# First FFN products of a hybrid decoder block: plain copies out of PSUM, and the row factor of x2 moved into a lane beside the next weights

## The chip, the core and the metric

The kernel runs on one core of a Trainium2 chip. The metric is the device time of one execution in microseconds. In the text PE is the matrix engine (TensorE), DVE the VectorE, ACT the ScalarE, POOL the GpSimd and SP the engine that issues most DMAs. The five engines run their own instruction streams in order and wait for each other through semaphores.

## What is computed

One layer of a decoder block on 256 rows of width 2048, fp32: a hybrid token mixer, cross-attention into 256 memory rows, and a gated MLP (FFN). Each has an RMSNorm before and after. The change lies where the second sub-layer ends and the FFN begins:

```python
x = x + rmsnorm(y, g[3])          # x2, end of the cross-attention
h = rmsnorm(x, g[4])
up = h @ w_up                      # 2048 x 11264
conv = conv_b + sum(up_pad[:, j:j + s] * conv_w[j] for j in range(3))
gate, val = jnp.split(conv, 2, axis=-1)
y = (jax.nn.gelu(gate) * val) @ w_down
x = x + rmsnorm(y, g[5])
```

The row factor of `rmsnorm(x, g[4])` is one number for each row, and `h @ w_up` is linear in the rows, so the kernel multiplies by it after the matmul.

## The kernel before

**Numbers and weights.** A weight block of 4 x 128 rows and 256 columns is loaded by SP into one of four `raw` buffers (512 KB). ACT makes the high half `hi` of it (L234, a cast) and DVE the rest `lo` (L236, a subtraction); both have three buffers. A product is then `hi` times x's high half, `hi` times x's low half and `lo` times x's high half. `split` gives these two instructions a high priority.

**The end of x2.** The four column chunks of x2 (tiles `row`) are finished by DVE (L1337). As they come, `transposed` turns each into `h3T` (tiles `h`): PE transposes into the PSUM tiles `auxp` and `auxq` (L389), ACT scales the high half out (L375), DVE the low half (L376). The row factor isn't in `h3T`. `row_factors` makes it: eight squares with row sums on ACT (L409), a reduce and a scaling on DVE (L412, L413), a power on POOL (L414). `over_rows` spreads it over all partitions: a small matmul on PE (L421) and a copy by DVE into `rrow` (L424), which the code calls `x2row`. The squares are pinned behind the last high half of `h3T`.

**The first FFN products.** `wstat_first` makes the first gate block and the first value block together, in all four banks of the PSUM tag `mm` (two row tiles each), with 192 matmuls of 256 columns at L287. It takes `h3T` step by step as the transposes give it. All later blocks come from `wstat2`, 16 steps for each of two row tiles: one matmul of 512 columns (L302) and one of 256 (L304) a step, in two banks. Call such a couple of matmuls a pair.

**Emptying the banks.** `conv` multiplies a product by `x2row` into `z` and applies the width-3 convolution, with one ACT and two DVE instructions (L1484, L1485, L1487). For the first two blocks the multiplication reads PSUM itself (L1479), so each of the four banks is held until `x2row` exists. For later blocks the two halves of a bank are added first (an ACT copy at L1481 and a DVE addition at L1482) and POOL multiplies by `x2row` (L1483). The gate goes through Gelu (L1497), is multiplied by the value (L1502) and split into `hid` (L1505, L1506).

**What sets the order.** The program is written in one stream; a scheduler of the framework orders each engine's instructions from it, with priorities (`tc.high_priority`). A `Lanes` object `L` holds generators: `L.add` puts work in, and the loops over weights call `L.advance`, which lets a lane issue its next piece behind the matmul just written (`tc.issue_after`). Before the change no lane runs during the FFN.

Of the kernel before, what the change touches and what calls it, by code (L numbers as in the profile page):

```python
# [15 lines left out]
AF = mybir.ActivationFunctionType  # L16
# [4 lines left out]
P = 128  # L21
D = 2048
S = 256
# [149 lines left out]
def hybrid_block(tc, a, out, dbg=None):  # L173
    nc = tc.nc
    dbg = dbg or {}
    with ExitStack() as ctx:
# [14 lines left out]
        def mk(pool, tag, bufs, shape=(P, 512), dt=F32):  # L191
            t = pool.tile(list(shape), dt, tag=tag, bufs=bufs, name=nm(tag))
            return t
# [207 lines left out]

        def row_factors(src, tmp, pins=(None,) * 4):

            r = mk(cp, "rs", 3, (P, 2))
            part = mk(cp, "rpart", 2, (P, 8))
            for c in range(4):
                with tc.issue_after(pins[c].ins) if pins[c] else ExitStack():
                    for t in range(2):
                        nc.scalar.activation(tmp(), src[t][c], AF.Square,  # L409
                                             accum_out=part[:, 4 * t + c:4 * t + c + 1])  # L410
            ss = small(2)
            nc.vector.tensor_reduce(ss, part.rearrange("p (t c) -> p t c", t=2), axis=AX.X, op=ALU.add)  # L412
            nc.vector.tensor_scalar(ss, ss, 1.0 / D, 1e-6, op0=ALU.mult, op1=ALU.add)  # L413
            last_pow[0] = nc.gpsimd.tensor_tensor(r, ss, mhalf[:, :2], op=ALU.pow)  # L414
            return r
# [1049 lines left out]
                    nc.sync.dma_start(dbg["x2"][t * P:(t + 1) * P, c * 512:(c + 1) * 512], x2[t][c])  # L1465


        x2row = over_rows(row_factors(x2, xtmp, (h3T.last,) * 4))
        right2.close()
        mixer.close()  # L1470
        ffn = ExitStack()
# [4 lines left out]
        def conv(ps, dst, n):  # L1476
            z = mk(fp, "z", 4, (P, S))
            if ps.shape[1] == S:
                nc.vector.tensor_tensor(z, ps, x2row, op=ALU.mult)  # L1479
            else:  # L1480
                nc.scalar.copy(z, ps[:, S:])  # L1481
                nc.vector.tensor_tensor(z, ps[:, :S], z, op=ALU.add)  # L1482
                nc.gpsimd.tensor_tensor(z, z, x2row, op=ALU.mult)  # L1483
            nc.scalar.activation(dst, z, AF.Identity, bias=cw[:, 3, n:n + 1], scale=cw[:, 2, n:n + 1])  # L1484
            nc.vector.scalar_tensor_tensor(dst[:, 1:], z[:, :S - 1], cw[:, 1, n:n + 1], dst[:, 1:],  # L1485
                                           op0=ALU.mult, op1=ALU.add)
            nc.vector.scalar_tensor_tensor(dst[:, 2:], z[:, :S - 2], cw[:, 0, n:n + 1], dst[:, 2:],  # L1487
                                           op0=ALU.mult, op1=ALU.add)

        hid = Packed(2)  # L1490
        first = wstat_first(w_up, (0, D_FF), 256, h3T)
        for j in range(FT // 2):
            g = mk(fp, "gv", 4)
            ps = wstat2(w_up, j * 256, 256, h3T) if j else first[0]
            for t in range(2):
                conv(ps[t], g[:, t * S:(t + 1) * S], 2 * j + t)
            nc.scalar.activation(g, g, AF.Gelu_apprx_tanh)  # L1497
            v = mk(fp, "gv", 4)
            ps = wstat2(w_up, D_FF + j * 256, 256, h3T) if j else first[1]
            for t in range(2):  # L1500
                conv(ps[t], v[:, t * S:(t + 1) * S], FT + 2 * j + t)
            nc.vector.tensor_tensor(v, v, g, op=ALU.mult)  # L1502
            hi = mk(fp, "hid", FT, dt=F32R)
            lo = mk(fp, "hid", FT, dt=F32R)
            nc.scalar.copy(hi, v)  # L1505
            nc.vector.tensor_tensor(lo, v, hi.bitcast(F32), op=ALU.subtract)  # L1506
            hid.hi.append(view(hi, k=2, t=S))
            hid.lo.append(view(lo, k=2, t=S))

        gb5 = bcast_row(gains[5], hbuf32)  # L1510

# [33 lines left out]
```

## Time and profile before

| | us |
|---|---|
| median of 3 runs | 1355.32 |
| lowest and highest of them | 1351.33, 1360.78 |
| the profiled execution, its own time | 1363.17 |
| span of its profile, first to last instruction | 1361.4 |
| PE busy | 1325.9 |
| DVE busy | 874.0 |
| ACT busy | 707.3 |

A row of the timeline gives the start, the time until the end, the engine and line, the tile written and the tiles read, the number of instructions merged, and in brackets how long the engine was idle before and what released it. Matmuls overlap, so PE's rate is read from the distance of starts. PEclk is the share of full clock that PE was granted: 1.00 is 2.4 GHz and 0.50 is 1.2 GHz. Times are from the start of the span. The FFN's first matmul starts at 604.77 us, and the last FFN matmul at about 1353 us.

### The profile page before, as it was taken

The numbers are of one execution on the slowest core, as the hardware profiler recorded it, in microseconds if no ns is written. First come the engines' busy times: TensorE is split into PE (matmuls) and PEld (weight loads), VectorE is DVE, ScalarE is ACT, GpSimd is POOL, SyncE is SP. The second block draws the span as 40 slices with busy tenths as digits, with TensorE's granted clock in tenths as the row PEclk, the third lists the DMA queues.
The fourth block names the chain that finished last, engine by engine and source line by source line (L and its number), as shares of the span: only waits on it lengthen the run. The fifth ranks groups of instructions, "written<-read, shape, count | busy, mean of one in ns | idle before, by whom it ended". The sixth has DMA issues, their size and how long they took to land.

```text
span 1361.4 us, 20945 instructions
## 1 busy us (share of the span) xinstructions
PE 1325.9 (97%) x8184; PEld 1160.2 (85%) x8184; DVE 874.0 (64%) x1298; ACT 707.3 (52%) x1075; POOL 141.6 (10%) x179
## 2 busy tenths in 40 slices
PE   6899999999999999989999999999999999999997
PEld 6889979989977889778888888888888888888886
DVE  6579964466775765566766767676767674444444
ACT  6755363244456654556555555555555553434442
POOL 3010101200013100000111111111111120000000
PEclk9999999999999999998999999999999999999999
DMA  7545553155558755444666566666666666666663
GB/s 236 143 138 156 148 171 101 48 178 155 148 162 298 232 178 174 155 124 140 184 186 187 186 186 186 186 185 186 186 186 186 187 217 198 191 196 192 195 194 132
DMA packets 189841, 238.82 MB, mean 175 GB/s; under 512 B 7920, under 2 KB 144013, under 8 KB 189741
## 3 DMA queue, kind: packets, MB, share of 16 engines
q1 hardware_dynamic: 185514, 225.23, 53.6%
q0 software_dynamic: 3376, 11.29, 2.5%
q8 instruction: 64, 1.05, 0.3%
q10 hardware_dynamic: 851, 0.95, 0.2%
q14 instruction: 36, 0.29, 0.1%
HBM read 235.33 MB, written 2.12 MB: 174 GB/s over the span
## 4 chain that ended last, share of the span: by engine, by line
PE 92%; DVE 2%; issue 2%; DMA 2%; ACT 1%; POOL 1%; ACTq 0%; SPq 0%; DVEq 0%; POOLq 0%
PE mm L302 23%; PE mm L304 12%; PE mm L324 11%; PE mm L330 11%; PE mm L326 11%; PE mm L271 5%; PE mm L266 5%; PE mm L268 5%; PE mm L287 1%; DMA wa<-in_rwkv_w_up_dram 1%; PE auxq L675 1%; DVE lo L236 1%; ACT hi L234 1%; PE auxp L1073 0%; PE auxq L933 0%
## 5 line engine op out<-in xcount | busy, mean ns | idle before, releaser
L236 DVE TENSOR_TENSOR lo<-raw,hi 128x1024 fp32r<-128x1024 f32 x422 | 519.6, 1233 | 380.8 <-ACT hi L234 378.9
L234 ACT CAST hi<-raw 128x1024 fp32r<-128x1024 f32 x422 | 442.9, 1050 | 452.8 <-PE mm L302 170.0
L302 PE MATMUL mm<-h,hi 128*128 128x512 f32 x1344 | 477.6, 400 | 2.4 <-DVE z L1479 2.4
L304 PE MATMUL mm<-h,lo 128*128 128x256 f32 x1344 | 378.7, 282 | 0.0
L302 PEld LDWEIGHTS mm<-h,hi 128*128 128x128 f32 x1344 | 253.9, 189 | 66.1 <-issue 2.5
L304 PEld LDWEIGHTS mm<-h,lo 128*128 128x128 f32 x1344 | 255.3, 190 | 0.0
L266 PE MATMUL mm<-h,hi 128*128 128x256 f32 x592 | 153.1, 290 | 0.0
L268 PE MATMUL mm<-h,hi 128*128 128x256 f32 x592 | 150.5, 286 | 0.0
L324 PE MATMUL mm<-hi,hid 128*128 128x512 f32 x352 | 137.0, 389 | 0.0
L326 PE MATMUL mm<-hi,hid 128*128 128x512 f32 x352 | 136.9, 389 | 0.0
L266 PEld LDWEIGHTS mm<-h,hi 128*128 128x128 f32 x592 | 113.9, 193 | 2.6 <-issue 1.5
L268 PEld LDWEIGHTS mm<-h,hi 128*128 128x128 f32 x592 | 113.8, 193 | 0.4 <-issue 0.3
L1483 POOL TENSOR_TENSOR z<-z,rrow 128x256 f32<-128x256 f32 x84 | 69.1, 823 | 412.1 <-DVE z L1482 412.1
L330 PE MATMUL mm<-lo,hid 128*128 128x512 f32 x352 | 108.4, 389 | 0.0
L271 PE MATMUL mm<-h,lo 128*128 128x256 f32 x592 | 97.5, 285 | 0.0
L271 PEld LDWEIGHTS mm<-h,lo 128*128 128x128 f32 x592 | 82.5, 192 | 1.3 <-DVE lo L236 0.6
L324 PE MATMUL mm<-hi,h 128*128 128x512 f32 (+1 forms) x208 | 79.2, 386 | 1.7 <-ACT hi L234 1.7
L326 PEld LDWEIGHTS mm<-hi,hid 128*128 128x128 f32 x352 | 66.1, 188 | 13.8
L330 PEld LDWEIGHTS mm<-lo,hid 128*128 128x128 f32 x352 | 66.1, 188 | 13.7
L324 PEld LDWEIGHTS mm<-hi,hid 128*128 128x128 f32 x352 | 66.0, 188 | 13.7
L326 PE MATMUL mm<-hi,h 128*128 128x512 f32 (+1 forms) x208 | 77.0, 375 | 0.0
L330 PE MATMUL mm<-lo,h 128*128 128x512 f32 (+1 forms) x208 | 59.8, 375 | 0.2 <-DVE lo L236 0.2
(347 smaller groups left out, 1545.2 us busy)
## 6 DMA issues: line engine op xcount, KB each, us to landing
raw<-in_ffn_w_up_dram SPq DMA_DIRECT2D x176, 512.0 KB, 4.6
raw<-in_w_in_dram SPq DMA_DIRECT2D x94, 512.0 KB, 4.3
raw<-in_ffn_w_down_dram SPq DMA_DIRECT2D x88, 512.0 KB, 4.9
raw<-in_w_out_dram SPq DMA_DIRECT2D x32, 512.0 KB, 4.7
raw<-in_mem_wkv_dram SPq DMA_DIRECT2D x16, 512.0 KB, 3.5
raw<-in_mem_wq_dram SPq DMA_DIRECT2D x8, 512.0 KB, 3.4
raw<-in_mem_wo_dram SPq DMA_DIRECT2D x8, 512.0 KB, 3.7
x<-in_x_dram SPq DMA_DIRECT2D x8, 256.0 KB, 6.8
```

What stands on the lines that cost most here:

```text
L234: nc.scalar.copy(hv, rv)
L236: nc.vector.tensor_tensor(lv, rv, hv.bitcast(F32), op=ALU.subtract)
L266: nc.tensor.matmul(o, lhsT=hv[:, k, cs], rhs=X.h(k0 + k), start=(k0 + k == 0), stop=False)
L268: nc.tensor.matmul(o, lhsT=hv[:, k, cs], rhs=X.l(k0 + k), start=False, stop=False)
L271: L.last = nc.tensor.matmul(o, lhsT=lv[:, k, cs], rhs=X.h(k0 + k), start=False, stop=(k0 + k == nk - 1))
L287: L.last = nc.tensor.matmul(ps[g][t][:, :S], lhsT=w[:, k, cs], rhs=x(k0 + k), start=(k0 + k == 0 and i == 0), stop=(k0 + k == KT - 1 and i ...
L302: nc.tensor.matmul(view(ps[t], z=2, t=S), lhsT=hv[:, k, cs], rhs=X.hl[k0 + k], start=(k0 + k == 0), stop=False)
L304: L.last = nc.tensor.matmul(ps[t][:, S:], lhsT=lv[:, k, cs], rhs=X.h(k0 + k), start=False, stop=(k0 + k == KT - 1))
L324: nc.tensor.matmul(o, lhsT=X.h(kk)[:, ts_], rhs=hv[:, k, :], start=(first and k0 + k == 0), stop=False)
L326: nc.tensor.matmul(o, lhsT=X.l(kk)[:, ts_], rhs=hv[:, k, :], start=False, stop=False)
L330: L.last = nc.tensor.matmul(o, lhsT=X.h(kk)[:, ts_], rhs=lv[:, k, :], start=False, stop=(last and k0 + k == nk - 1))
L1483: nc.gpsimd.tensor_tensor(z, z, x2row, op=ALU.mult)
```

## The change

`row_factors` is cut in two, so that `factors_of` (reduce, scaling, power) can follow squares made elsewhere. The eight squares of x2, the factor, `over_rows` and the whole first gated tile (`conv` of four products, Gelu, product, split) become a lane, `second_norm` with `first_hidden`, which is added before `wstat_first` and drained after the first `wstat2` block. The squares write their unused output into one tile `junk` of the FFN's pool instead of four rotating ones. The four products of `wstat_first` are copied from PSUM to new tiles `zf`, two by ACT and two by DVE, without the factor; `conv` then multiplies `zf` by the factor in SBUF. The arithmetic is the same.

```diff
         def row_factors(src, tmp, pins=(None,) * 4):
-            r = mk(cp, "rs", 3, (P, 2))
             part = mk(cp, "rpart", 2, (P, 8))
...
+            return factors_of(part)
+
+        def factors_of(part):
+            r = mk(cp, "rs", 3, (P, 2))
             ss = small(2)
...
-        x2row = over_rows(row_factors(x2, xtmp, (h3T.last,) * 4))
+        rpart = mk(cp, "rpart", 2, (P, 8))
+
+        def second_norm():
+
+            junk = mk(fp, "gv", 4)
+            for c in range(4):
+                for t in range(2):
+                    nc.scalar.activation(junk, x2[t][c], AF.Square, accum_out=rpart[:, 4 * t + c:4 * t + c + 1])
+                yield 2.2
+            got["x2row"] = over_rows(factors_of(rpart))
+            yield 1.0
+            yield from first_hidden()
...
         def conv(ps, dst, n):
             z = mk(fp, "z", 4, (P, S))
             if ps.shape[1] == S:
-                nc.vector.tensor_tensor(z, ps, x2row, op=ALU.mult)
+                nc.vector.tensor_tensor(z, ps, got["x2row"], op=ALU.mult)
...
-        first = wstat_first(w_up, (0, D_FF), 256, h3T)
-        for j in range(FT // 2):
-            g = mk(fp, "gv", 4)
-            ps = wstat2(w_up, j * 256, 256, h3T) if j else first[0]
...
+        def first_hidden():
+            gv = [mk(fp, "gv", 4) for _ in range(2)]
+            for n in range(2):
+                for t in range(2):
+                    conv(got["first"][n][t], gv[n][:, t * S:(t + 1) * S], n * FT + t)
+                yield 1.5
+            nc.scalar.activation(gv[0], gv[0], AF.Gelu_apprx_tanh)
+            hidden(0, *gv)
+
+        L.add(second_norm())
+        first = wstat_first(w_up, (0, D_FF), 256, h3T)
+        with tc.high_priority(offset=2 * AHEAD):
+            got["first"] = [[mk(fp, "zf", 4, (P, S)) for _ in range(2)] for _ in range(2)]
+            for n in range(2):
+                for t in range(2):
+                    copy2(t, got["first"][n][t], first[n][t])
+        for j in range(1, FT // 2):
+            g = mk(fp, "gv", 4)
+            ps = wstat2(w_up, j * 256, 256, h3T)
+            if j == 1:
+                L.drain(lambda: not L.lanes)
```

`copy2` is an older helper: a DVE copy (L733 of the new file) where its first argument is odd, an ACT copy (L735) where it is even.

What the scheduler makes of it, first on PE where `wstat_first` ends and the first `wstat2` block begins. Before (`auxp` with `rs` is `over_rows`; `mm_6444` to `mm_6447` are the four first products, and `mm_6717` takes the bank of `mm_6444`):

```order
L287 MATMUL mm_6447<-h_6407,hi_6636 128x256 x2
L287 MATMUL mm_6447<-h_6407,lo_6637 128x256
L421 MATMUL auxp_6434<-ident,rs_6412 128x128 x2
L302 MATMUL mm_6717<-h_6323,hi_6721 128x512
L304 MATMUL mm_6717<-h_6323,lo_6722 128x256
```

The same place of the changed kernel (`mm_6418` to `mm_6421` are the first products, and `mm_6680` and `mm_6681` take the banks of the first two):

```order
L287 MATMUL mm_6421<-h_6407,lo_6618 128x256
L302 MATMUL mm_6680<-h_6323,hi_6684 128x512
L304 MATMUL mm_6680<-h_6323,lo_6685 128x256
...
L302 MATMUL mm_6681<-h_6337,hi_6684 128x512
L304 MATMUL mm_6681<-h_6337,lo_6685 128x256
L424 MATMUL auxp_6709<-ident,rs_6704 128x128 x2
L302 MATMUL mm_6680<-h_6347,hi_6716 128x512
```

The matmul of `over_rows` (now L424) has moved behind the first eight pairs of the next block.

On DVE at the same place, before (`small` is the factor on its way, `rrow` its spread form):

```order
L236 TENSOR_TENSOR lo_6722<-raw_6719,hi_6721 128x1024
L412 TENSOR_REDUCE small_6430<-rpart_6413 128x2
L413 TENSOR_SCALAR small_6430<-small_6430 128x2
L236 TENSOR_TENSOR lo_6744<-raw_6741,hi_6743 128x1024
L236 TENSOR_TENSOR lo_6766<-raw_6763,hi_6765 128x1024
L424 COPY rrow_6437<-auxp_6434 128x256
L1479 TENSOR_TENSOR z_6689<-mm_6444,rrow_6437 128x256
```

And on DVE after:

```order
L236 TENSOR_TENSOR lo_6685<-raw_6682,hi_6684 128x1024
L415 TENSOR_REDUCE small_6705<-rpart_6412 128x2
L416 TENSOR_SCALAR small_6705<-small_6705 128x2
L733 COPY zf_6672<-mm_6419 128x256
L733 COPY zf_6674<-mm_6421 128x256
L236 TENSOR_TENSOR lo_6717<-raw_6714,hi_6716 128x1024
L236 TENSOR_TENSOR lo_6751<-raw_6748,hi_6750 128x1024
L427 COPY rrow_6712<-auxp_6709 128x256
L236 TENSOR_TENSOR lo_6783<-raw_6780,hi_6782 128x1024
L1494 TENSOR_TENSOR z_6730<-zf_6671,rrow_6712 128x256
```

The DVE copies stand behind the reduce, and the multiplication by the factor stands behind the low halves of the next block.

On ACT, after, where the squares end (before, all eight squares stood behind the last `h` row, with two casts behind the second of them; two now stand ahead of that row):

```order
L375 ACTIVATE h_6407<-auxq_6401,gpar 128x256
L1478 ACTIVATE gv_6482,rpart_6412<-row_6204 128x512
L1478 ACTIVATE gv_6482,rpart_6412<-row_6208 128x512
L234 CAST hi_6617<-raw_6615 128x1024
L234 CAST hi_6684<-raw_6682 128x1024
...
L1478 ACTIVATE gv_6482,rpart_6412<-row_6306 128x512
L735 COPY zf_6671<-mm_6418 128x256
L234 CAST hi_6716<-raw_6714 128x1024
L735 COPY zf_6673<-mm_6420 128x256
```

The first ACT copy stands behind all eight squares, with nothing between it and the last of them.

## Rows read from the trace of the kernel before

**Rows 1.** The page's head and its row of PE: span, and PE's busy time with its share of the span.

```profile
span 1361.4 us, 20945 instructions
PE 1325.9 (97%) x8184; PEld 1160.2 (85%) x8184; DVE 874.0 (64%) x1298; ACT 707.3 (52%) x1075; POOL 141.6 (10%) x179
```

**Rows 2.** All waits of PE from 604 us to the end of the span: who waited for whom, us in total, times, longest.

```profile
PE auxp L389 <- DVE row L1337: 2.9, 1, 2.9
PE mm L302 <- DVE z L1479: 2.4, 1, 2.4
PE auxp L421 <- POOL rs L414: 0.5, 1, 0.5
PE mm L287 <- ACT h L375: 0.3, 1, 0.3
```

**Rows 3.** Timeline of PE where the first FFN products end and the next block begins.

```profile
631.91 0.40 PE L287 MATMUL mm<-h,hi 128*128 128x256 f32 x2
632.15 0.28 PE L287 MATMUL mm<-h,lo 128*128 128x256 f32 x1
632.92 0.71 PE L421 MATMUL auxp<-ident,rs 128*128 128x128 f32 x4 [0.49 <-POOL rs L414]
636.01 0.77 PE L302 MATMUL mm<-h,hi 128*128 128x512 f32 x1 [2.38 <-DVE z L1479]
636.78 0.63 PE L302 MATMUL mm<-h,hi 128*128 128x512 f32 x1
...
641.91 0.48 PE L302 MATMUL mm<-h,hi 128*128 128x512 f32 x1
...
642.35 0.40 PE L302 MATMUL mm<-h,hi 128*128 128x512 f32 x1
...
643.75 0.40 PE L302 MATMUL mm<-h,hi 128*128 128x512 f32 x1
```

**Rows 4.** Busy time of each engine in stretches (columns: stretch and its length, PE, PEld, DVE, ACT, POOL busy with instructions, then PEclk, DMA share, GB/s): around the pause of rows 3, and two stretches earlier in the FFN's first products.

```profile
605.00:610.00 5.00, 5.00 (x32) 5.00 (x33) 2.92 (x6) 1.79 (x4) 0.00 (x0) 0.71 0.16 56
620.00:625.00 5.00, 4.90 (x41) 4.70 (x40) 4.01 (x7) 3.51 (x8) 0.00 (x0) 1.00 0.37 113
...
634.00:635.00 1.00, 0.00 (x0) 0.00 (x0) 1.00 (x2) 0.00 (x0) 0.00 (x0) 1.00 0.05 9
635.00:636.00 1.00, 0.00 (x0) 0.02 (x1) 0.97 (x4) 0.05 (x1) 0.00 (x0) 0.63 0.68 172
636.00:637.00 1.00, 0.99 (x3) 0.91 (x4) 0.94 (x4) 1.00 (x3) 0.00 (x0) 0.50 1.04 352
...
641.00:642.00 1.00, 1.00 (x5) 0.85 (x4) 0.00 (x0) 0.71 (x1) 0.00 (x0) 0.50 0.00 0
642.00:643.00 1.00, 1.00 (x7) 0.86 (x7) 0.63 (x1) 0.98 (x2) 0.00 (x0) 0.96 0.00 0
```

**Rows 5.** Timeline of ACT from the last steps of `h3T` to the first convolution: the transposed halves, the squares with the reading of their sums, the casts.

```profile
616.95 0.47 ACT L375 ACTIVATE h<-auxq,gpar 128x256 fp32r<-128x256 f32 x1
619.36 1.05 ACT L234 CAST hi<-raw 128x1024 fp32r<-128x1024 f32 x1 [1.94 <-issue]
...
624.42 0.47 ACT L375 ACTIVATE h<-auxq,gpar 128x256 fp32r<-128x256 f32 x1 [1.08 <-DVE h L376]
624.79 0.62 ACT L409 ACTIVATE tmp<-row 128x512 f32<-128x512 f32 x1
625.31 0.19 ACT L409 ACTIVATION_READ_ACCUMULATOR tmp<-row 128x1 f32 x1
625.40 0.62 ACT L409 ACTIVATE tmp<-row 128x512 f32<-128x512 f32 x1
...
631.50 0.19 ACT L409 ACTIVATION_READ_ACCUMULATOR tmp<-row 128x1 f32 x1
631.63 1.99 ACT L234 CAST hi<-raw 128x1024 fp32r<-128x1024 f32 x2
```

**Rows 6.** Timeline of DVE from the reduce of the squares to the first multiplication by the factor.

```profile
631.72 0.16 DVE L412 TENSOR_REDUCE small<-rpart 128x2 f32<-128x8 f32 x1 [2.28 <-ACT tmp L409]
...
632.71 2.36 DVE L236 TENSOR_TENSOR lo<-raw,hi 128x1024 fp32r<-128x1024 f32 x2 [0.62 <-ACT hi L234]
634.99 0.42 DVE L424 COPY rrow<-auxp 128x256 f32<-128x256 f32 x1
635.44 1.09 DVE L1479 TENSOR_TENSOR z<-mm,rrow 128x256 f32<-128x256 f32 x3
```

**Rows 7.** Groups of instructions from 660 to 1000 us, the steady FFN: line, engine, operation, tiles and shapes, count, busy us, mean ns of one, idle time before and its releaser.

```profile
L302 PE MATMUL mm<-h,hi 128*128 128x512 f32 x964 | 340.7, 399 | 0.0
...
L236 DVE TENSOR_TENSOR lo<-raw,hi 128x1024 fp32r<-128x1024 f32 x121 | 148.3, 1225 | 103.3 <-ACT hi L234 103.3
...
L1484 ACT ACTIVATE gv<-z,cw 128x256 f32<-128x256 f32 x60 | 36.0, 600 | 5.6 <-POOL z L1483 5.6
L1487 DVE SCALAR_TENSOR_TENSOR gv<-z,cw,gv 128x254 f32<-128x254 f32 x60 | 28.7, 479 | 1.1
...
L1482 DVE TENSOR_TENSOR z<-mm,z 128x256 f32<-128x256 f32 x60 | 25.1, 418 | 0.0
L1481 ACT COPY z<-mm 128x256 f32<-128x256 f32 x61 | 22.1, 363 | 14.9 <-PE mm L304 14.9
```

**Rows 8.** Busy time of each engine in 100 us of the steady FFN (columns as in rows 4).

```profile
700.00:800.00 100.00, 100.00 (x568) 86.68 (x568) 68.86 (x97) 57.01 (x80) 13.93 (x17) 1.00 0.61 187
```

More of the change, by code (lines that the diff above doesn't have):

```diff
@@ L1482, in conv @@
                 nc.vector.tensor_tensor(z, ps[:, :S], z, op=ALU.add)
-                nc.gpsimd.tensor_tensor(z, z, x2row, op=ALU.mult)
+                nc.gpsimd.tensor_tensor(z, z, got["x2row"], op=ALU.mult)
             nc.scalar.activation(dst, z, AF.Identity, bias=cw[:, 3, n:n + 1], scale=cw[:, 2, n:n + 1])
@@ L1490, in hybrid_block, with hidden @@
         hid = Packed(2)
-        first = wstat_first(w_up, (0, D_FF), 256, h3T)
-        for j in range(FT // 2):
-            g = mk(fp, "gv", 4)
-            ps = wstat2(w_up, j * 256, 256, h3T) if j else first[0]
[L1495 to L1501, printed above, removed]
+        hid.hi = [None] * (FT // 2)
+        hid.lo = [None] * (FT // 2)
+        def hidden(j, g, v):
             nc.vector.tensor_tensor(v, v, g, op=ALU.mult)
@@ L1506, in hybrid_block @@
             nc.vector.tensor_tensor(lo, v, hi.bitcast(F32), op=ALU.subtract)
-            hid.hi.append(view(hi, k=2, t=S))
-            hid.lo.append(view(lo, k=2, t=S))
+            hid.hi[j] = view(hi, k=2, t=S)
+            hid.lo[j] = view(lo, k=2, t=S)
+        def first_hidden():
[18 more added lines that the diff above has]
+                L.drain(lambda: not L.lanes)
+            for t in range(2):
+                conv(ps[t], g[:, t * S:(t + 1) * S], 2 * j + t)
+            nc.scalar.activation(g, g, AF.Gelu_apprx_tanh)
+            v = mk(fp, "gv", 4)
+            ps = wstat2(w_up, D_FF + j * 256, 256, h3T)
+            for t in range(2):
+                conv(ps[t], v[:, t * S:(t + 1) * S], FT + 2 * j + t)
+            hidden(j, g, v)
         gb5 = bcast_row(gains[5], hbuf32)
```

## The prediction

> **What bounds the kernel now.** I read the head of the page first: PE is busy for 1325.9 of 1361.4 us, 97% [rows 1]. So the time goes down only where PE stands still or runs slowly. Next I read PE's waits from the start of the FFN to the end of the span. There are only four, and one belongs to this change: 2.4 us before L302, ended by the multiplication by the factor, after 0.5 us for the factor itself [rows 2]. From there on PE waits for nobody: L302 shows no idle time in the steady FFN [rows 7], and PE is busy for 100.00 of 100 us there [rows 8]. So whatever PE saves at this place reaches the end of the kernel in full.
>
> PE's timeline shows the place. Two L287 matmuls start from 631.91 on and the last at 632.15, so they follow each other at 0.12 us, and the last leaves PE free at about 632.27. The small matmul of `over_rows` starts at 632.92 and fills 0.71 us, to 633.63. The next block starts at 636.01 [rows 3]. PE stands still for 0.65 + 2.38 = 3.03 us.
>
> A second loss hangs on the first. The windows show a granted clock of 1.00 until 635, 0.63 in the next microsecond, 0.50 from 636 to 642, then 0.96 [rows 4]: the lower level, 1.2 GHz, in the first six microseconds after the pause. In rows 3 the pairs start 0.65 to 0.77 us apart at first (636.01, 636.78), and 0.35 us apart at the end, since four pairs lie between 642.35 and 643.75, (643.75 - 642.35) / 4. Ten pairs ran from 636.01 to 642.35, in 6.34 us; at 0.35 us they take 3.50. The slow clock costs 2.84 us.
>
> Why the pause is so long is seen on ACT and DVE. Eight squares stand behind the last high half of `h3T` and two casts among them, so the last sum is read at 631.50 to 631.69 [rows 5]. The reduce starts at 631.72; then two low halves hold DVE from 632.71 to 635.07, the copy of the spread factor starts at 634.99, the first multiplication at 635.44 [rows 6]. Only that frees a bank.
>
> **The change, part by part.**
>
> *The banks.* Each of the four banks is now freed by a copy that needs no factor. The bank of the first product is complete nine matmuls before the last L287: 632.15 - 9 x 0.12 = 631.07, plus a length of 0.28 us [rows 3], 631.35. The ACT copy is like the copy at L1481, 0.363 us [rows 7]: done at about 631.75, 0.5 us before PE is free at 632.27. The second bank goes to DVE, whose copy is like L1482 with one operand fewer, at most 0.418 us [rows 7]: complete at 631.7, copied by 632.2, and needed only by the ninth matmul of the block, at 632.27 + 4 x 0.35 = 633.7. So the wait for the banks goes. The four copies are new work, 2 x 0.363 + 2 x 0.418 = 1.56 us, on engines that are free for 43 and 31 of 100 us [rows 8]; they lie beside PE's pairs. Without this cover they would cost 1.56 us.
>
> The page "VectorE: DVE Perf Modes" of the Trainium skill, section "Rules for kernel authors", advises to let an elementwise operation read the matmul's output directly, or to copy it to SBUF first if many operations follow. Here a single one follows, so by that rule the copies are only added work, 1.56 us off the gain that is summed below. The wait in rows 2 speaks for the copies at no cost: it is the bank that PE waits for, which the rule doesn't ask about.
>
> *The squares.* All eight must be over before the first copy, as nothing lies between on ACT. Before, they end at 631.69. Two now stand ahead of the last high half: the first falls in the 1.94 us that ACT is idle before 619.36, the other before 624.42, where ACT is idle for 1.08 us [rows 5]. So six follow instead of eight: 2 x 0.61 us less (the distance of 624.79 and 625.40, [rows 5]), 630.5 us. Against that, all write one tile now, so a square may wait until the sum of the one before is stored, 0.10 us more each (625.31 + 0.19 = 625.50 instead of 625.40): 0.6 us at most. And the first square and two `h` halves now precede a cast that ran at 619.36; in the new order of PE its low half is needed eleven matmuls later than before, so I cost this on PE at nothing, but ACT's later work can slip by up to 1 us. Bounds for the last sum: 630.5 and 632.1. I take 631.0, before the copy could start anyway (631.35). At the late end the copy is done at 632.5 and PE waits 0.2 us. The cover is then gone: each further tenth costs a tenth.
>
> *The matmul of `over_rows`* stands behind eight pairs, 632.27 + 8 x 0.35 = 635.1, when its factor is long there (before, 1.2 us passed from the last sum to this matmul). I keep its 0.71 us in the sum.
>
> *The lane's first gated tile.* Its work ran in the pause. Now it lies between the low halves of coming weights, in DVE's queue. A unit of weights is eight pairs, 2.80 us of PE, against 1.225 us for the low half [rows 7]. From 632.27 to the end of two blocks (64 pairs, 22.4 us) DVE has eight low halves (9.8), two copies, five factor steps (7 x 0.418 = 2.9), twelve convolution steps (12 x 0.479 = 5.7) and about two larger products (1.4 by the length of 0.7 that twice the elements suggest): 19.8 us at full lengths, with overlap less. It fits. The tightest place is the low half for the second block's first unit: it follows the spread factor (635.8), one low half (637.1), four multiplications (638.8), and three convolution steps that wait for ACT's 0.600 us [rows 7] (640.6), so it ends at 641.8. PE needs it after 32 pairs and `over_rows`, 632.27 + 11.2 + 0.71 = 644.2. Slack 2.4 us. SP's queue gets nothing new, and DVE frees `raw` buffers no later than PE needs the next, four units (11.2 us) on.
>
> *Sum.* Before, PE reaches the eleventh pair at 642.35. After: 632.27 + 0.71 + 10 x 0.35 = 636.48, at full clock, since no pause precedes. The gain is 5.87 us, 3.03 of pause and 2.84 of clock. On the profiled execution's own time: 1363.17 - 5.87 = 1357.3. That execution lies 7.85 us above the median of the runs shown, so I take the difference off the median: 1355.32 - 5.87 = **1349.4 us**, 0.4% less. A change of about 1% is what a measurement of this kernel can tell from none (its three runs differ by 9.45 us), so by that bound this is "the same".
>
> **The rivals.**
>
> *The copies come onto the path* (late squares, or PE waiting for all of the emptying). The 1.56 us are then paid: gain 4.31, time 1351.0. For it: ACT's margin is only 0.5 us. Against: PE's first pairs need one bank. Chance 0.12.
>
> *The clock falls all the same.* Then only the pause of 3.03 us is won: 1352.3. Against: from 620 to 625 PE has a wait of 0.3 us and the clock is 1.00 [rows 2, 4]; the lower level shows only behind 2.9 us (0.71 from 605 to 610) and behind the pause of rows 3. The steady FFN cycles four banks at 1.00 [rows 8]. Chance 0.05. The Trainium skill's page "TensorE: Matmul & The Clock Gate" tells, in the section "A second HAM failure mode: psum-queue depth-cycling", of a kernel that cycles PSUM banks and has its clock swing because of small pauses between groups. With that rule the trace does not agree so far.
>
> *The lane starves PE: slower.* DVE's queue is in order. If the first gated tile goes through it in one piece ahead of the second block's low half, four multiplications, eight steps and ACT's four (4 x 0.418 + 8 x 0.479 + 4 x 0.600 = 7.9 us), less the slack of 2.4, leave a new pause of 5.5, and with it the slow clock of 2.84: 8.3 - 5.87 = 2.5 us lost, 1357.8. It decides from a lateness of 2.4 + 3.0 us on. For it: DVE gets more work where it has a deadline. Against: the order puts a low half after every three to five steps. Chance 0.05.
>
> *It does nothing:* another wait, such as the cast of the next weights, ends at 636 too. Before, that cast (631.63) stands behind the squares, and its weights are there; after, it can start at 631.8, and is needed at 635.8. Chance 0.02, with 1355.3.
>
> **How the numbers follow.** 0.76 for the forecast, 1349.4. Two things widen it: the terms (1 us) and the scatter of the runs, -4.0 to +5.5 us around their median. That gives 1345 to 1355; the rivals above lie between 1351.0 and 1357.8, so I take 1344 to 1356.5, which leaves out about 2 in 10. Faster by over 1% means under 1341.8: no case reaches it, only scatter, 0.03. Slower by over 1% means over 1368.9: only several new pauses, 0.02. Within 1%: 0.95.
>
> **What would show it.** Right: after the last L287 the next L302 starts within 0.2 us, a bank copy precedes it, the clock stays at 1.00 from 610 to 650, pairs are 0.35 us apart from the start, and no new wait of PE appears up to 700 us. The squares' part is wrong if PE waits there for an ACT copy; the lane's part if L302 waits for DVE's low half around 644 to 655. The forecast is wrong if a new pause of over 2 us shows, or if time is lost in stages that the change doesn't touch.

## The result, and the profile after

The changed kernel took 1350.14 us (median of 19 runs, 1346.60 to 1354.96), beside 1356.15 for the kernel before in the same job (19 runs, 1351.33 to 1366.12). The ratio is 0.9938 with a 95% interval of [0.9921, 0.9955]: a gain of 0.6%, clear of no change by its interval but under the bound of 1%. The profiled execution took 1352.56 us. Its page begins:

```profile
span 1350.8 us, 20948 instructions
PE 1317.6 (98%) x8184; PEld 1157.1 (86%) x8184; DVE 873.6 (65%) x1300; ACT 708.3 (52%) x1077; POOL 143.9 (11%) x179
```

PE is busy for 8.3 us less than in [rows 1], with as many instructions. The waits of PE from 600 us to the end, beside [rows 2]:

```profile
PE auxp L389 <- DVE row L1340: 3.2, 2, 2.9
PE mm L287 <- ACT h L375: 0.3, 1, 0.3
```

The waits at L302 and L421 are gone, and none is new: the second wait at L389, of 0.27 us, lies ahead of the FFN, and the kernel before has it too (at 599.75, outside the window of [rows 2]). The timeline of PE at the place, beside [rows 3], and the last pair of the up-projection:

```profile
636.74 0.28 PE L287 MATMUL mm<-h,lo 128*128 128x256 f32 x1
636.86 0.40 PE L302 MATMUL mm<-h,hi 128*128 128x512 f32 x1
...
639.33 0.40 PE L302 MATMUL mm<-h,hi 128*128 128x512 f32 x1
639.57 0.28 PE L304 MATMUL mm<-h,lo 128*128 128x256 f32 x1
639.69 0.60 PE L424 MATMUL auxp<-ident,rs 128*128 128x128 f32 x4
640.05 0.47 PE L302 MATMUL mm<-h,hi 128*128 128x512 f32 x1
...
640.83 0.39 PE L302 MATMUL mm<-h,hi 128*128 128x512 f32 x1
...
1102.93 0.40 PE L302 MATMUL mm<-h,hi 128*128 128x512 f32 x1
```

The first L302 starts 0.12 us behind the last L287, and the eleventh (640.83) 4.09 us behind it; before, that took 642.35 - 632.15 = 10.20 us [rows 3]. The place gains 6.11 us. The windows around it, and 100 us of the steady FFN, beside [rows 4] and [rows 8]:

```profile
636.00:637.00 1.00, 1.00 (x10) 1.00 (x9) 0.42 (x1) 1.00 (x2) 0.26 (x1) 1.00 0.86 293
637.00:638.00 1.00, 1.00 (x8) 0.86 (x7) 0.94 (x2) 1.00 (x3) 0.00 (x0) 1.00 0.52 181
641.00:642.00 1.00, 1.00 (x7) 0.87 (x7) 1.00 (x2) 0.00 (x0) 0.00 (x0) 1.00 0.94 283
...
700.00:800.00 100.00, 100.00 (x579) 87.43 (x578) 70.92 (x100) 58.60 (x82) 14.91 (x18) 1.00 0.61 190
```

The granted clock stays at 1.00 around the place. The last row holds something that was not looked for: at the same clock, and busy for the same 100.00 us, PE does 579 matmuls instead of 568. The group of L302 from 660 to 1000 us says the same, 394 ns instead of 399 [rows 7]:

```profile
L302 PE MATMUL mm<-h,hi 128*128 128x512 f32 x982 | 340.5, 394 | 0.0
```

From the eleventh pair to the last, the 1344th, it is 1102.93 - 640.83 = 462.10 us, 0.3467 us a pair. Before, the last pair started at 1113.33:

```profile
1113.33 0.40 PE L302 MATMUL mm<-h,hi 128*128 128x512 f32 x1
```

1113.33 - 642.35 = 470.98 us, 0.3533 us a pair. That is 8.88 us more than the place gives, and the diff holds nothing that makes a matmul quicker. I call 0.3533 the loose rhythm and 0.3467 the tight one. In the loose one the distances repeat every three pairs (0.361, 0.349, 0.350); in the tight one they alternate (0.350, 0.343) or are all 0.347. The changed kernel starts its first eight pairs in the loose rhythm, (639.33 - 636.86) / 7 = 0.353 us, and has the tight one behind the small matmul of `over_rows`. The two profiles add up: FFN start to end of span, 1361.4 - 604.77 = 756.6 us before and 1350.8 - 609.24 = 741.6 after, 15.1 us less, of which 6.11 + 8.88 make 15.0. The spans differ by only 10.6, because that execution of the changed kernel reached the FFN 4.5 us later, in stages that the change leaves alone.

The single runs of the kernel before fall into two groups, which fits the two rhythms. Over the four jobs of this study it ran 78 times: 39 runs lie under 1358.5 us (mean 1354.45) and 39 above (mean 1363.29), 8.84 us apart, about the 8.88 above. The profiled execution of before, 1363.17 us, is one of the upper group, and loose. Only profiled executions show their rhythm; for the others it is inferred from the time. The 31 runs of the changed kernel are one group (mean 1350.01).

### The profile page after: what moved, and what is told of

Its sections match the earlier page's. It is cut to its first block, busy times and chain, and to the rows that moved or that the text cites. A ratio compares the mean times of both kernels' runs of the same rounds, so it can differ in the third digit from the quotient of the medians.

```text
span 1350.8 us, 20948 instructions
## 1 busy us (share of the span) xinstructions
PE 1317.6 (98%) x8184; PEld 1157.1 (86%) x8184; DVE 873.6 (65%) x1300; ACT 708.3 (52%) x1077; POOL 143.9 (11%) x179
## 4 chain that ended last, share of the span: by engine, by line
PE 93%; DVE 2%; issue 1%; DMA 1%; ACT 1%; POOL 1%; ACTq 0%; DVEq 0%; POOLq 0%
PE mm L302 23%; PE mm L304 11%; PE mm L324 11%; PE mm L326 11%; PE mm L330 11%; PE mm L271 6%; PE mm L266 5%; PE mm L268 5%; PE mm L287 2%; DMA wa<-in_rwkv_w_up_dram 1%; PE auxq L678 1%; DVE lo L236 1%; DMA raw<-in_w_in_dram 0%; PE auxp L389 0%; PE auxq L389 0%
## 5 line engine op out<-in xcount | busy, mean ns | idle before, releaser
L302 PE MATMUL mm<-h,hi 128*128 128x512 f32 x1344 | 466.2, 394 | 0.0
L304 PE MATMUL mm<-h,lo 128*128 128x256 f32 x1344 | 372.3, 277 | 0.0
L302 PEld LDWEIGHTS mm<-h,hi 128*128 128x128 f32 x1344 | 252.0, 188 | 58.6
L266 PE MATMUL mm<-h,hi 128*128 128x256 f32 x592 | 155.2, 293 | 1.6 <-ACT h L375 1.6
L268 PE MATMUL mm<-h,hi 128*128 128x256 f32 x592 | 152.3, 288 | 0.0
L271 PE MATMUL mm<-h,lo 128*128 128x256 f32 x592 | 99.1, 289 | 0.0
```

Source lines behind the costliest of these rows:

```text
L266: nc.tensor.matmul(o, lhsT=hv[:, k, cs], rhs=X.h(k0 + k), start=(k0 + k == 0), stop=False)
L268: nc.tensor.matmul(o, lhsT=hv[:, k, cs], rhs=X.l(k0 + k), start=False, stop=False)
L271: L.last = nc.tensor.matmul(o, lhsT=lv[:, k, cs], rhs=X.h(k0 + k), start=False, stop=(k0 + k == nk - 1))
L302: nc.tensor.matmul(view(ps[t], z=2, t=S), lhsT=hv[:, k, cs], rhs=X.hl[k0 + k], start=(k0 + k == 0), stop=False)
L304: L.last = nc.tensor.matmul(ps[t][:, S:], lhsT=lv[:, k, cs], rhs=X.h(k0 + k), start=False, stop=(k0 + k == KT - 1))
```

## The experiments

Two theories of the place were at stake: that the copies alone end the wait (the banks), or that the squares, done earlier, count too. And of the rhythm: A, a small matmul between two pairs brings the tight rhythm; B, chance draws it in each execution; C, the placement in SBUF sets it. Later: F, small matmuls turn either rhythm into the other; R, any interruption draws it anew; S, the place where the small matmul stands decides. Where three numbers stand together below, they are the distances in PE's timeline from the last L287 to the first L302 and to the eleventh, and the mean distance of pairs behind that.

**e1: the kernel before, unchanged.**

> The kernel before, unchanged, profiled a second time. In its first profile the pairs of matmuls of the FFN's up-projection (L302 and L304) started 0.3533 us apart from the second block to the last; in the changed kernel 0.354 us in the first eight pairs and 0.3467 us from the over_rows matmul on. Theory A (the small matmul put between the pairs shifts the rhythm of the stream, and it stays shifted): 0.3533 us again, and a pause of about 3 us with the clock at 0.50 behind it. Rival B (each execution falls into one of two rhythms by chance when the stream starts): 0.3533 or 0.3467 us, with about 9 us between such executions, the same pause. Rival C (the placement of tiles in SBUF sets it): 0.3533 us.

1364.17 us. 3.86 us, 8.95 us, 0.353 us: the loose rhythm again, in a run of the upper group. The pause is that of before to the hundredth, but ten pairs behind it took 5.09 us instead of 6.34, so the price of the clock varies from run to run. Theories A, B and C all allow this rhythm; the run doesn't tell them apart.

**e2: the copies alone.**

```diff
         first = wstat_first(w_up, (0, D_FF), 256, h3T)
+        with tc.high_priority(offset=2 * AHEAD):
+            zf = [[mk(fp, "zf", 4, (P, S)) for _ in range(2)] for _ in range(2)]
+            for n in range(2):
+                for t in range(2):
+                    copy2(t, zf[n][t], first[n][t])
+        first = zf
```

> The four plain copies out of PSUM alone; squares, factor and first gated tile stay where they were, with over_rows directly behind the last L287. My theory (the banks held for the factor make the pause): the first L302 starts about 0.1 us behind over_rows; of the 3.03 us of pause about 0.7 us stay, ahead of over_rows, the clock stays at 1.00, and the place gains 5.1 of the 5.9 us. Rival (the late squares make it): the ACT copy stands behind the squares and one cast, is late by 1 to 2 us, and the gain is under 3 us. For the pace: A and C 0.3533 us all along, since no small matmul stands between pairs; B either.

1357.58 us median (1347.95 to 1362.66, 10 runs), ratio 0.9984 [0.9950, 1.0018]. 1.23 us, 4.85 us, 0.353 us. The wait for the multiplication is gone and the clock stays up; what remains is `over_rows`, with its wait for the factor:

```profile
631.73 0.71 PE L421 MATMUL auxp<-ident,rs 128*128 128x128 f32 x4 [0.48 <-POOL rs L414]
632.20 0.48 PE L302 MATMUL mm<-h,hi 128*128 128x512 f32 x1
```

The copies alone give 10.20 - 4.85 = 5.35 of the 6.11 us at the place. But nine of the ten runs lie from 1356.38 to 1362.66; by their times the rhythm is loose nearly always, where the kernel before has it in about half its runs (15 of 25 beside e2). That hides the gain in the ratio: the nine have a mean of 1358.45, 5.0 us under the 1363.49 of the upper group beside them, close to the 5.35 at the place.

**e3: the lane alone** (the changed kernel without `zf`; `conv` reads the banks).

```diff
         first = wstat_first(w_up, (0, D_FF), 256, h3T)
-        with tc.high_priority(offset=2 * AHEAD):
-            got["first"] = [[mk(fp, "zf", 4, (P, S)) for _ in range(2)] for _ in range(2)]
-            for n in range(2):
-                for t in range(2):
-                    copy2(t, got["first"][n][t], first[n][t])
+        got["first"] = first
+        L.drain(lambda: not L.lanes)
...
-            if j == 1:
-                L.drain(lambda: not L.lanes)
```

> The lane of squares, factor and first gated tile without the plain copies: the first products stay in PSUM until they are multiplied by the factor, and the lane is drained ahead of the next block. My theory: the factor is ready about 1 us earlier, the 0.65 us ahead of over_rows go, but DVE's two low halves still stand ahead of the spread factor; the pause shrinks by 0.5 to 1.5 us and the clock still falls to 0.50 behind it: gain 0.5 to 1.5 us. Rival (the squares are what holds the banks): the pause falls under 1 us, the clock stays, and the gain is 4 us or more. Pace: 0.3533 us by A.

1357.62 us median (1351.72 to 1368.51, 10 runs in two groups of five), ratio 0.9977 [0.9938, 1.0015]. 3.86 us, 10.02 us, 0.353 us: the pause is not a hundredth shorter, where I had expected 0.5 to 1.5 us less. The timelines of PE and DVE tell why:

```profile
637.84 0.28 PE L287 MATMUL mm<-h,lo 128*128 128x256 f32 x1
637.96 0.60 PE L424 MATMUL auxp<-ident,rs 128*128 128x128 f32 x4
641.70 0.77 PE L302 MATMUL mm<-h,hi 128*128 128x512 f32 x1 [3.14 <-DVE z L1494]
```

```profile
636.22 0.16 DVE L415 TENSOR_REDUCE small<-rpart 128x2 f32<-128x8 f32 x1 [1.48 <-ACT gv L1478]
636.41 0.17 DVE L416 TENSOR_SCALAR small<-small 128x2 f32<-128x2 f32 x1
638.40 2.36 DVE L236 TENSOR_TENSOR lo<-raw,hi 128x1024 fp32r<-128x1024 f32 x2 [1.82 <-ACT hi L234]
640.68 0.42 DVE L427 COPY rrow<-auxp 128x256 f32<-128x256 f32 x1
641.13 1.09 DVE L1494 TENSOR_TENSOR z<-mm,rrow 128x256 f32<-128x256 f32 x3
```

The squares are done earlier: the reduce starts 1.62 us ahead of the last L287, where before it started 0.43 us ahead [rows 3, 6]. `over_rows` waits for nothing. Yet the multiplication starts 641.13 - 637.84 = 3.29 us behind the last L287, as before (635.44 - 632.15 = 3.29). Between stand two low halves on DVE, and they wait for ACT's cast, which itself waited 1.14 us for PE here:

```profile
637.32 1.99 ACT L234 CAST hi<-raw 128x1024 fp32r<-128x1024 f32 x2 [1.14 <-PE mm L287]
```

That cast starts 0.52 us ahead of the last L287 in the kernel before as well (632.15 - 631.63 [rows 3, 5]), where the last sum is read until 631.69. The way from there to the first L302 has the same steps in both, which is why the pause is the same to the hundredth. So the factor was not what PE waited for, but DVE's queue, in which `rrow`'s copy stands behind two low halves of weights that PE needs only later. No run puts that copy ahead of the low halves with the banks still held, so what this alone would give isn't shown. Of the two changes, the copies and the lane, only the copies shorten the pause; with them, the lane takes the factor's wait off as well (4.85 to 4.09 us).

**e7: PE kept busy in the pause of the kernel before** (eight matmuls into an unused bank, behind `over_rows`).

```diff
+                x2row_mm[0] = nc.tensor.matmul(ps[:, t * P:(t + 1) * P], lhsT=r[:, t:t + 1].to_broadcast([P, P]), rhs=ident,
...
         first = wstat_first(w_up, (0, D_FF), 256, h3T)
+        warm = auxq()
+        with tc.issue_after(x2row_mm[0].ins):
+            for k in range(8):
+                nc.tensor.matmul(view(warm, z=2, t=S), lhsT=h3T.h(k)[:, :P], rhs=h3T.hl[k], start=True, stop=True)
```

> The kernel before, with eight matmuls of 512 columns, read by nobody, behind over_rows' in the pause that the multiplies leave (2.38 us). The pause itself stays; TensorE works through some 1.8 us of it. If the half clock behind the pause comes from the idleness, the granted clock stays 1.00, and from the first pair to the eleventh it takes 3.5 us instead of 6.34: a gain of 2.84 us at the place, as the prediction has that term. If the clock falls for another reason (the wait by itself, or the change of shapes), the eleventh pair comes 6.3 us behind the first, as before. The time as a whole, a single one, goes by the rhythm of the run: 1353 or 1361.

1354.63 us, one run. 3.86 us, 7.41 us, 0.347 us. The pause is the same to the hundredth, and PE now works through most of it:

```profile
636.19 0.71 PE L423 MATMUL auxp<-ident,rs 128*128 128x128 f32 x4 [0.49 <-POOL rs L414]
636.66 2.10 PE L1497 MATMUL auxq<-h 128*128 128x512 f32 x8
639.29 0.47 PE L302 MATMUL mm<-h,hi 128*128 128x512 f32 x1 [0.53 <-DVE z L1481]
```

The granted clock is 1.00 throughout:

```profile
638.00:639.00 1.00, 0.76 (x4) 0.28 (x2) 0.97 (x3) 0.00 (x0) 0.00 (x0) 1.00 0.53 130
...
640.00:641.00 1.00, 1.00 (x8) 0.87 (x7) 1.00 (x4) 1.00 (x3) 0.00 (x0) 1.00 0.73 186
```

The ten pairs take 7.41 - 3.86 = 3.55 us instead of 6.34: 2.79 us, where the prediction has 2.84. So it was the idle time that cost the clock; e8 and e10 show the same at another pause.

**e4: the kernel before, with a second spread of the factor behind the twelfth pair, read by nobody.**

```diff
-        x2row = over_rows(row_factors(x2, xtmp, (h3T.last,) * 4))
+        x2r = row_factors(x2, xtmp, (h3T.last,) * 4)
+        x2row = over_rows(x2r)
...
+        def tick():
+            yield 2.0
+            ps = auxp()
+            for t in range(2):
+                nc.tensor.matmul(ps[:, t * P:(t + 1) * P], lhsT=x2r[:, t:t + 1].to_broadcast([P, P]), rhs=ident,
+                                 start=True, stop=True)
+            yield 0.0
...
+            if j == 1:
+                L.add(tick())
             ps = wstat2(w_up, j * 256, 256, h3T) if j else first[0]
+            if j == 1:
+                L.drain(lambda: not L.lanes)
```

> The kernel before with one more spread of the factor (two small matmuls into a PSUM tile that nobody reads) between the twelfth and the thirteenth pair of the next block; nothing else is changed. Theory A: the pairs behind it start 0.3467 us apart to the end of the up-projection, about 1330 x 0.0067 = 8.9 us less, minus 0.4 us for the added matmuls, with the pause as before. Rivals B and C: no change of pace at that place; the time of the kernel before or 0.4 us more.

1356.77 us median (1352.82 to 1367.64, 10 runs, eight of them under 1359), ratio 0.9981 [0.9948, 1.0014]. The profiled run (1363.11 us) goes against A: its pairs are 0.347 us apart ahead of the small matmuls and 0.353 from there to the end, so the small matmul brought the loose rhythm there.

**e5: the copies alone, with that spread behind the eighth pair** (the copies as in e2; `tick` as in e4, with its first `yield` as argument).

```diff
...
+            if j == 1:
+                L.add(tick(1.0))
...
```

> The copies alone (as in e2), and two small matmuls (a spread of the factor, read by nobody) behind exactly eight pairs of the up-projection, where the changed kernel has its own. Theory F: the pairs of an unbroken stream begin 0.3533 us apart, and small matmuls between two pairs take them from 0.3533 to 0.3467 or back: every run is then 1326 pairs x 6.67 ns = 8.8 us below e2's runs at 0.3533 (mean 1358.5), about 1349.7, and the profile shows 0.3467 from the ninth pair on. Theory R: what interrupts the stream only draws the rhythm anew: the runs fall in two groups, about 1349.7 and 1358.5, with members in both. Theory C (what counts is where the tiles lie in SBUF, which is e2's): nothing changes, nine runs of ten at 1358.5.

1350.68 us median (1350.38 to 1352.00, 4 runs), ratio 0.9916 [0.9887, 0.9945]. Two more small matmuls than e2, and 6.9 us less by the medians (of different jobs). The profile has 1.24 us, 5.24 us, 0.3467 us. But it was tight ahead of the spread as well (distances of 0.350 and 0.344), so a spread doesn't always turn the rhythm over, as F has it. It also means that this profile doesn't show the spread making the rhythm tight; the four times fit F, but their cause isn't shown.

**e6: the changed kernel, with a spread behind the 136th pair.**

```diff
...
+            if j == 3:
+                L.add(tick(1.0))
...
```

> The changed kernel with a second pair of small matmuls, read by nobody, behind the 136th pair of the up-projection. Theory F (they take the pairs from one rhythm to the other): 0.3467 us before and 0.3533 us behind them, 1198 pairs x 6.67 ns = 8.0 us more in every run, about 1358.1. Theory R (the rhythm is drawn anew): two groups, 1350.1 and 1358.1, with members in both. Theory A (small matmuls bring the faster rhythm, whichever was there): 1350.2 in all runs.

1356.88 us median (1355.46 to 1360.83, 10 runs), ratio 0.9985 [0.9961, 1.0010]. The mean, 1357.73, is 7.7 us above the changed kernel's, where 8.0 was worked out. None of the ten runs is near 1350: against A, and against R, which wants both groups. The profile shows 0.3467 us up to the 136th pair and 0.3533 behind it; its windows ahead of and behind the spread:

```profile
650.00:680.00 30.00, 30.00 (x175) 26.24 (x174) 22.45 (x32) 17.67 (x26) 5.86 (x7) 1.00 0.62 192
700.00:800.00 100.00, 100.00 (x569) 86.73 (x567) 69.46 (x98) 57.98 (x80) 14.86 (x18) 1.00 0.58 185
```

That is 5.83 and 5.69 matmuls a microsecond.

**e12: the changed kernel, with spreads behind the 136th and the 584th pair.**

```diff
...
+            if j in (3, 10):
+                L.add(tick(1.0))
...
```

> The changed kernel with two further pairs of small matmuls, read by nobody: behind the 136th pair of the up-projection (as in e6) and behind the 584th. Theory F (each turns the rhythm over): the profile shows 0.3467 us up to the 136th pair, 0.3533 from there to the 584th, and 0.3467 to the end; 448 pairs x 6.67 ns = 3.0 us above the changed kernel, about 1353. Theory S (behind the 136th pair something else, such as where the weights then lie, makes the slower rhythm, and it stays): 0.3533 to the end, about 1358.

1352.68 us, one run. The windows of its profile:

```profile
690.00:790.00 100.00, 100.00 (x568) 86.72 (x567) 68.78 (x97) 57.98 (x80) 14.53 (x18) 1.00 0.60 186
...
860.00:960.00 100.00, 100.00 (x579) 88.27 (x578) 71.36 (x100) 58.97 (x82) 14.95 (x19) 1.00 0.61 190
960.00:1060.00 100.00, 100.00 (x579) 88.20 (x578) 70.14 (x98) 58.85 (x82) 14.79 (x18) 1.00 0.62 190
```

568 matmuls in 100 us between the two spreads, 579 behind the second, at a clock of 1.00. So neither rhythm belongs to the weights that follow or to a place in SBUF (C and S as a lasting cause): within one execution it changes at such a spread and holds until the next. In none of the fourteen profiles does it change anywhere else behind the twelfth pair. What decides which way it goes is open. Behind the eighth pair it was tight in every profile that has a spread there (from loose in seven, from tight in e5's), behind the 136th loose, behind the 584th tight, and behind e4's twelfth loose in the profile.

**e9: the changed kernel, unchanged, in the job of the next two.**

> The changed kernel once more, unchanged, for more of its runs, on the chip on which the next two run. Theory F (the up-projection starts at 0.3533 us and over_rows' matmuls take it to 0.3467, in every run): one group of runs, 1347 to 1355, median about 1350, the profile with 0.3467 from the ninth pair on; none near 1359. Theory R (the rhythm is drawn in each execution, and nineteen runs were luck): some runs near 1359.

1349.70 us median (1347.51 to 1353.00, 12 runs), ratio 0.9940 [0.9914, 0.9965]. One group; 0.12 us, 4.09 us, 0.3467 us, as in its first profile, with the first eight pairs loose.

**e8: the changed kernel, with PE kept busy in the earlier pause** of 2.9 us at L389, behind which the clock was 0.66 from 610 to 615 us (before, 0.71 from 605 to 610 [rows 4]).

```diff
                 take(c, ps)
+            warm = auxq()
+            with tc.issue_after(L.last.ins), tc.high_priority(offset=2 * AHEAD):
+                for k in range(8):
+                    nc.tensor.matmul(warm, lhsT=vm[0][:, :P], rhs=vm[1][:, :512], start=True, stop=True)
```

> The changed kernel with eight matmuls of 512 columns, read by nobody, in the earlier pause of 2.9 us ahead of the feed-forward's first transposes, behind which the granted clock was 0.66 for 5 us. If idleness is what costs the clock, the first L287 matmuls come 0.12 us apart from the start instead of 0.215: 23 of them, 23 x 0.095 = 2.2 us less at the place, and about 1347.9 in all. If the 1.0 us that stays idle is enough to lose the clock, or the extra matmuls hold up the transposes: no gain, 1350.1 or up to 1 us more.

1349.49 us median (1348.90 to 1353.26, 5 runs), ratio 0.9920 [0.9880, 0.9959]. The clock is 1.00 from 600 to 625 us, but the filler is longer than the pause:

```profile
603.47 7.03 PE L1451 MATMUL auxq<-v,v 128*128 128x512 f32 x16
610.33 0.38 PE L389 MATMUL auxp<-ident,row 128*128 128x128 f32 x2
```

Each of the eight is two instructions on plain float32 and takes 7.03 / 8 = 0.88 us, about four times what the expectation counts with (1.9 us for all eight, 0.24 each). The L389 matmul waits for the filler now, and what the clock gives is paid back: the five runs have a mean of 1350.81 us, beside 1350.01 for the changed kernel.

**e10: the same with three of them** (`range(3)`).

> As e8, with three matmuls of plain float32 in place of eight: at the 0.88 us that each took in e8's profile they fill 2.6 us of the earlier pause of 2.9 us and should hold nothing up. If e8's clock (1.00 behind the pause) is kept, 23 L287 matmuls come 0.12 us apart instead of 0.215: 2.2 us less than the changed kernel in the same job, about 1348 to its 1350. If the little that stays idle or the later transposes take it back: equal within 0.5 us.

1346.99 us median (1346.10 to 1351.24, 9 runs), ratio 0.9925 [0.9899, 0.9952], beside e9's 1349.70 in the same job: 2.7 us less by the medians and 2.1 by the means (1347.74 and 1349.85), where 2.2 was worked out. The timeline of PE, and a window behind the pause:

```profile
600.25 2.73 PE L1451 MATMUL auxq<-v,v 128*128 128x512 f32 x6
602.82 0.38 PE L389 MATMUL auxq<-ident,row 128*128 128x128 f32 x2
...
605.19 0.28 PE L287 MATMUL mm<-h,hi 128*128 128x256 f32 x1
605.31 0.28 PE L287 MATMUL mm<-h,lo 128*128 128x256 f32 x1
...
605.00:610.00 5.00, 5.00 (x44) 4.97 (x44) 3.58 (x8) 2.35 (x6) 0.00 (x0) 1.00 0.11 38
```

The L287 matmuls start 0.12 us apart right behind the pause; in the changed kernel they were 0.215 apart there (610.21, 610.42, 610.64) until 614. From the FFN's first matmul to the last L287 it is 25.99 us here, 27.74 in e9's profile and 27.50 in the first of the changed kernel. The intervals of e9 and e10 against the kernel before overlap; compared with each other, their means differ by 2.1 us with a 95% interval of 0.5 to 3.7, so e10 is quicker.

**e11: the squares into two tiles in turn** instead of one.

```diff
-            junk = mk(fp, "gv", 4)
+            junk = [mk(fp, "gv", 4) for _ in range(2)]
...
-                    nc.scalar.activation(junk, x2[t][c], AF.Square, accum_out=rpart[:, 4 * t + c:4 * t + c + 1])
+                    nc.scalar.activation(junk[t], x2[t][c], AF.Square, accum_out=rpart[:, 4 * t + c:4 * t + c + 1])
```

> The changed kernel with the lane's eight squares written to two tiles in turn instead of one. If ScalarE's wait for its own last write of the same tile makes the squares 0.75 us apart (0.615 before, into several tiles), they come 0.615 us apart again, the eighth some 0.9 us earlier against the products around it; if the instruction itself is slower here (what it reads, or a neighbour on the SBUF), they stay 0.75 apart. In neither case does the time move (the copies of the banks wait for TensorE, not for ScalarE): 1350 within its runs.

1348.43 us, one run. ACT's timeline at the last squares, in the changed kernel:

```profile
633.61 0.63 ACT L1478 ACTIVATE gv<-row 128x512 f32<-128x512 f32 x1
634.14 0.19 ACT L1478 ACTIVATION_READ_ACCUMULATOR gv<-row 128x1 f32 x1
634.36 0.63 ACT L1478 ACTIVATE gv<-row 128x512 f32<-128x512 f32 x1
634.90 0.19 ACT L1478 ACTIVATION_READ_ACCUMULATOR gv<-row 128x1 f32 x1
635.98 0.37 ACT L735 COPY zf<-mm 128x256 f32<-128x256 f32 x1 [0.89 <-PE mm L287]
```

and with two tiles:

```profile
629.08 0.63 ACT L1478 ACTIVATE gv<-row 128x512 f32<-128x512 f32 x1
629.60 0.20 ACT L1478 ACTIVATION_READ_ACCUMULATOR gv<-row 128x1 f32 x1
629.69 0.63 ACT L1478 ACTIVATE gv<-row 128x512 f32<-128x512 f32 x1
630.21 0.20 ACT L1478 ACTIVATION_READ_ACCUMULATOR gv<-row 128x1 f32 x1
631.89 0.37 ACT L735 COPY zf<-mm 128x256 f32<-128x256 f32 x1 [1.48 <-PE mm L287]
```

The squares start 0.75 us apart into one tile and 0.61 into two. One tile costs each square about 0.14 us, and it costs the kernel nothing, as the copy waits for PE either way; ACT's margin grows from 0.89 to 1.48 us, by 0.6 where 0.9 was expected.

## Why the prediction was right, and where not

**The number.** 1349.4 was predicted and 1350.14 measured, and the range held it. Part of this agreement is luck: the sum was taken off a median, 1355.32, the middle of three runs, two of the lower group and one of the upper. It happens to lie 0.9 us above the lower group's mean. Against that group's mean the changed kernel gains 1354.45 - 1350.01 = 4.4 us, against the upper group's 1363.29 - 1350.01 = 13.3 us; 5.87 was predicted for every run. With the rhythm's 8.88 taken off, the upper group gives 4.4 as well, so by the times the sum was about 1.5 us too high.

**The banks: right.** The copies alone did 5.35 of 6.11 us (e2). The ACT copy ended at 635.98 + 0.37 = 636.35, 0.5 us before PE's first L302 at 636.86, the margin that was worked out.

**The pause, 3.03 us: right in size, and its cause half wrong.** That the pause is so long was put down to the squares first, and then to the two low halves. In e3 the low halves, and the cast ahead of them that waits for PE, hold it without the squares: with the sums over a microsecond earlier it lasted as long. The part on the squares therefore gains nothing by itself.

**The clock, 2.84 us: the mechanism right, the size that of one execution.** e7 measured 2.79 with PE kept busy. Across four profiles with the pause (before, e1, e3, e4) the eleventh L302 came 10.20, 8.95, 10.02 and 8.97 us behind the last L287, so the change is worth 4.9 to 6.1 us at the place, with the rhythm aside, and the 2.84 is the dearest of the four slow clocks (2.84, 1.59, 2.66 and 1.61 us over 3.50 for the ten pairs). The lower group's 4.4 lies a little below; no execution of the unchanged kernel in that group was profiled, so the rest is open.

**Squares and their tile: right within the bounds.** 0.14 us a square where up to 0.10 was allowed, but they started early enough: the last sum was there at 635.09, 1.65 us ahead of the last L287, the early end of the bounds (632.15 - 630.5), and ACT then waited 0.89 us for PE.

**`over_rows`: too dear.** 0.71 us were kept. Here it starts at 639.69, just when a pair was due, and the next pair at 640.05; with the 0.43 us to the pair behind that one, it costs 0.36 + 0.08 = 0.44 us. That 0.27 covers the difference between 5.87 and 6.11; the ten pairs themselves took 0.03 more than 3.50.

**The lane: right.** DVE took the factor steps and convolutions between low halves, and PE waited for none up to the end. No rival came true: the copies were not on the path, and the clock did not fall at the place. One of the named signs didn't hold as worded: the clock was 0.66 from 610 to 615 us, not 1.00, because this execution reached the FFN 4.5 us later and that window lies behind the earlier pause of 2.9 us.

**The rule on banks.** The Trainium skill's page "VectorE: DVE Perf Modes", section "Rules for kernel authors", would leave the copies out, since a single operation follows. e2 and e3 differ from it: without the copies the lane gained no pause back, and the copies alone took it from 3.86 to 1.23 us, 2.6 us less, on engines with time to spare.

**What the prediction lacked: the rhythm of the pairs.** It took 0.35 us a pair from a few rows, before and after alike. The 0.0067 us between the rhythms were worth 8.88 us over 1333 pairs, more than all terms of the sum. By the times, the changed kernel is tight in all its 31 runs, the kernel before in about half. In every one of the seven profiles of the changed kernel and its variants the rhythm turns from loose to tight at the matmul of `over_rows`, so this comes from where it now stands. The times of e2 and e5 agree: with the copies but `over_rows` ahead of the first pair the runs were loose (9 of 10), with small matmuls behind the eighth pair they were tight (4 of 4), though e5's one profile was tight before them. Why this matmul turns the rhythm to tight there, and others elsewhere to loose, stays open. The means, 1358.87 us in 78 runs before and 1350.01 in 31 after, differ by 8.9 us, 0.65%: about 4.4 are the place, and about 4.4 are half of 8.88, for the loose half of the runs that is gone. The second part was neither foreseen nor, as far as the diff shows, aimed at.

## What to carry to other kernels

When a wait ends on a chain, look at the queue of the engine that ends it before shortening the chain: here the factor was early enough, and low halves that nobody needed yet stood ahead of its copy. Emptying PSUM with a plain copy pays where PE waits for the bank and the copying engines have time; and a pause of a few microseconds is paid twice, so count the clock behind it, or fill what can't be removed with matmuls no longer than the pause. Plot the single runs before subtracting from a median: where they form two groups, a change can win or lose by moving runs from one to the other, as here about half of the gain.

## What the runs showed of the hardware

- A stream of pairs (512 and 256 columns, each with its own weights) holds one of two rhythms at a granted clock of 1.00: 0.3467 or 0.3533 us a pair, over hundreds of pairs. Two small matmuls between pairs changed it in either direction (e4, e6, e12), and once not at all (e5). By the times, the outcome of such a spread within a stream that runs on was the same in every run of a kernel (the changed kernel 31 of 31, e6 10 of 10, e5 4 of 4; in e4, with the pause close ahead, eight of ten lie in the lower group). Behind a stop of 0.5 us and no spread it was loose in nine of ten (e2), behind the pause of the kernel before about even (39 of 78). What sets it stays open.
- A matmul of 512 columns on plain float32 took two instructions and 0.88 us (e8), against one instruction and 2.10 / 8 = 0.26 us for those of e7, whose operands ACT and DVE write as fp32r ([rows 5]).
- ACT squares with a row sum came 0.75 us apart into one tile and 0.61 into two in turn (e11).
- A stop of about 0.6 us (e2) or 0.5 us (e7) left the clock at 1.00; those of 2.4 and 2.9 us brought it to 1.2 GHz (0.50 in [rows 4], and from 605 to 610 us in e9) for up to six microseconds. Matmuls that nobody reads in the same pauses kept it at 1.00 (e7, e8, e10). Behind one and the same pause of 3.86 us, ten pairs took from 5.09 to 6.34 us in four profiles.
